# Projecting GQA's gate beside GQA's own attention instead of beside MLA's

## The chip, the cores and the metric

The kernel is one program on one core of a Trainium2 chip. The core has a matrix engine (TensorE, here PE, whose weight loads are shown apart as PEld), a vector engine (DVE), a scalar engine for activations and copies (ACT), a general engine (POOL) and a sync engine that issues the transfers (SP). Each engine works through its own list of instructions; semaphores make one wait for another. The metric is device time in microseconds (us) of one execution.

## The reference, cut to what matters

Two requests (512 and 256 tokens, width 1024) go through two layers with the same weights. Each layer norms its input, projects it, runs four groups of heads side by side, multiplies each group by its own SiLU gate, and projects the result back. All is float32.

```
h = rms_norm(x, norm_g) * (1 + scale) + shift        # scale, shift, gate from ada_w: "ada"
z = h @ w_in                                          # the four groups' inputs and gates ga..gd
oa = mla_branch(...)      # MLA: latents qa, kva -> normed -> up-projected q, k, v; 4 heads
ob = diff_branch(...)     # differential attention
oc = rglru_branch(...)    # recurrence
od = gqa_branch(...)      # GQA: 4 query heads on 2 key heads
o = concat([oa * silu(ga), ob * silu(gb), oc * silu(gc), od * silu(gd)])
x + gate * (o @ w_out)
```

The part that matters here: `od`, its gate `gd`, and MLA's latents and up-projections. `gd` is 256 columns of `w_in`, so a [tokens x 1024] by [1024 x 256] product.

## The kernel before, in words

Every float32 product is made of three products of halves (high and low parts of each operand), by `mm3` (line 286), so almost all matmuls of the profile stand on that line. They write PSUM tiles named acc, s, tr and pv. ACT's copies and activations all stand on line 115 (a helper).

A layer runs in this order. (1) `token_chunk(0)` and `token_chunk(1)` project GQA's q, k, v. (2) GQA's attention: eight jobs (two token groups, four heads), each of them scores into an s tile (L704, L705), row maximum on DVE (L521, L523), exponential on ACT (p<-s,mx), scaling by the row sum, transposes on PE (L538), copies of them to SBUF (pt<-tr), and the product with v (L545). (3) MLA's attention, the same with longer scores (L286, s<-b,b). (4) Recurrence and the differential heads' projections. (5) Differential attention with the other three gates. (6) The output projection.

PE would stand still in an attention while ACT and DVE work on exponentials, so `weave` mixes in other work: a generator `fill`, from which a number of steps is taken after each piece of a job (`F_D` for GQA's attention, `F_A` for MLA's, one number for each layer; `DUE_A` is the starting balance). What is left over is issued behind the attention by `take(fill)`.

- Beside GQA's attention, `fill` is `mla(...)`: six steps of `token_chunk(5)`, the latents of one tile of 128 tokens each, and then six steps that project a tile up (v, then q with its rotation). At the sixth latent step (`UP_AT`) the up-projection's weights wuq and wukv are loaded and split.
- Beside MLA's attention, `fill` is `mixed((3,))`: `gates(3)`, the gate of GQA, in four steps (two halves m of the columns, two token groups), with one chunk of `ada` after each two of them.

`gates(br)` loads and splits the weights of a half (`feat_load`: two transfers, each with an ACT copy into a wh tile and a subtraction on POOL or DVE into a wl tile), makes 24 matmuls for each token group (512 or 256 columns), and evacuates: a tanh on ACT, a scalar_tensor_tensor on DVE, and a multiplication by the attention's output. If the attention's output isn't there yet, the gate is kept in a tile and `gate_mul` multiplies later; the number of DVE operations is the same. wh and wl are pools of six tiles each, acc of two, ws of four; a pool hands out its tiles in the order in which the code asks for them.

The order in which an engine runs its instructions isn't the code's. `arrange` takes the whole program and lists it again: at each step the instruction, on any engine, that could start first by its own table of costs, and among equals the one that comes first in the code. So moving a step in the code changes its rank and the turn of its tiles, and `arrange` then settles where its instructions stand on each engine.

Of the kernel before, what the change touches and what calls it, by code (L numbers as in the profile page):

```python
# [34 lines left out]
GO_D, GO_A, GO_B = ((0, 1), (0, 1), (0, 1))  # L35
KORD = (6, 7, 4, 5, 0, 1, 2, 3)

F_D, F_A, F_B, F_C = ((0.897, 1.178), (0.494, 0.213), (1.2, 1.393), (1.833, 0.976))
MIX_A, MIX_B = (((3,), (3,)), ((0, 2, 1), (2, 0, 1)))
SPL = ((3, 0), (0, 0), (2, 0), None, (3, 1), (0, 1), (2, 1))  # L40
LATE = (3, 4)
LAG_D, LAG_A, LAG_B = ((1, 1), (1, 1), (1, 2))
# [3 lines left out]
PRE_D, PRE_A, PRE_B, UP_AT = ((0, 0), (0, 0), (0, 0), (5, 5))  # L46
# [28 lines left out]
def body(ctx, tc, I, O, dbg=None):  # L75
# [8 lines left out]
    def sb(shape, dt=F32, tag=None, bufs=None):  # L84
        cnt[0] += 1
        nm = f"{tag or 'c'}_{cnt[0]}"
        tag = tag or nm
        return pool.tile(list(shape), dt, name=nm, tag=tag, bufs=bufs or BUFS.get(tag, 1))
# [5 lines left out]
    def ps(tag):  # L94
        cnt[0] += 1
        if tag == "acc":
            rot_acc.append(rot_acc.pop(0))
            tag = rot_acc[-1]
        return ppool.tile([P, 512], F32, name=f"{tag}_{cnt[0]}", tag=tag, bufs=PBUFS[tag])

    def gt(g, box, dt=F32R):

        if g == 0:
            return sb([P, 512], dt, tag="b")
        if not box:
            t = sb([P, 2, 256], dt, tag="b")
            box.extend([t[:, 1], t[:, 0]])
        return box.pop()
# [5 lines left out]
    def act(out, in_, f=AF.Copy, **kw):  # L114
        return nc.scalar.activation(out, in_, f, **kw)  # L115
# [105 lines left out]
    def ada_chunk(l, j, evac, deep):  # L221

        acc = ps("acc")
        for k in range(KC):
            w = deep[j][k] if deep else ada_load(l, j, k, ADA_T[k])
            c = 32 * (k % 4)
            nc.tensor.matmul(acc[c:c + 32], cs[:, k], w, start=(k < 4), stop=(k >= 4))
        evac(acc)
# [23 lines left out]
    def ada_gate(l):  # L252

        for j in range(2):
            c = slice(j * 512, (j + 1) * 512)

            def evac(acc):
                b2 = sb([2, 512], tag="t5")
                nc.sync.dma_start(b2, I["adabg"][l, :, c].to_broadcast([2, 512]))
                row = sb([P, 512], tag="tmp")  # L260
                V.tensor_copy(row, acc)
                rows = ps("acc")
                nc.tensor.matmul(rows[:2], sum4, row, start=True, stop=True)
                V.tensor_tensor(b2, rows[:2], b2, op=ALU.add)
                nc.sync.dma_start(gd[2 * l:2 * l + 2, c], b2)
            ada_chunk(l, 4 + j, evac, None)
            yield

    def load_split(src, n, kg, ncol, tl="wl", th="wh", eng="g"):

        his, los = [], []
        for q in range(n):
            w = sb([P, kg, ncol], tag="ws")
            nc.sync.dma_start(w, src(q))
            hi, lo = split_w(w, [P, kg, ncol], th, tl, eng)
            his.append(hi)
            los.append(lo)
        return his, los
# [91 lines left out]
    for step in START:  # L370
# [8 lines left out]
        else:  # L379
            _, g, hf = step  # L380
# [7 lines left out]
    for l in range(DEPTH):  # L388
# [33 lines left out]
        def token_load(ci):  # L422
            ncol = TCH[ci][1]
            base = sum(c for _, c in TCH[:ci]) * KC
            return load_split(
                lambda q: I["wt"][l, :, base + q * 2 * ncol:base + (q + 1) * 2 * ncol].rearrange(
                    "p (k c) -> p k c", k=2), 4, 2, ncol, eng=EN_T)
# [15 lines left out]
        def feat_load(m):  # L443
            return load_split(
                lambda q: I["wf"][l, m, :, q * 512:(q + 1) * 512].rearrange("p (k c) -> p k c", k=4), 2, 4, P, eng=EN_F)

        def feat_tile(m, evac, loaded=None):

            his, los = loaded or feat_load(m)
            for g, (t0, n) in enumerate(GRP):  # L450
                acc = ps("acc")
                hh, hl = H[g]
                for k in range(KC):
                    mm3(acc[:, :n], his[k // 4][:, k % 4], los[k // 4][:, k % 4], hh[k], hl[k], k == 0, k == KC - 1, "s")
                evac(g, t0, n, acc)
                yield
# [11 lines left out]
        def gate_in(k, g):  # L468
            return og[g][k]


        def gates(br, ahead):
            boxes = [], []
            w = feat_load(2 + 2 * br)
            for m in range(2):
                def evac(g, t0, n, acc):
                    t = sb([P, 512], tag="tmp")
                    act(t[:, :n], acc[:, :n], AF.Tanh, scale=0.5)
                    d = gate_in(2 * br + m, g)
                    if d is None:  # L480
                        d = og[g][2 * br + m] = gt(g, boxes[g], F32)
                        V.scalar_tensor_tensor(d, t[:, :n], 1.0, acc[:, :n], op0=ALU.add, op1=ALU.mult)
                    else:
                        V.scalar_tensor_tensor(t[:, :n], t[:, :n], 1.0, acc[:, :n], op0=ALU.add, op1=ALU.mult)  # L484
                        V.tensor_tensor(d, d, t[:, :n], op=ALU.mult)
                for i, _ in enumerate(feat_tile(2 + 2 * br + m, evac, w)):
                    if i == 0 and m == 0 and ahead:
                        w = feat_load(2 + 2 * br + 1)
                    yield
                if m == 0 and not ahead:  # L490
                    w = feat_load(2 + 2 * br + 1)
# [523 lines left out]
        def split_o(br, g):  # L1015
            f = 0.25 if br == 2 else 0.5
            for k in (2 * br, 2 * br + 1):
                hi, lo, o = *pair(g), og[g][k]
                act(hi, o, AF.Copy, scale=f)
                V.scalar_tensor_tensor(lo, o, f, hi.bitcast(F32), op0=ALU.mult, op1=ALU.subtract)  # L1020
                O2[g][k] = hi, lo
                yield
# [16 lines left out]
        def chain(*gens):  # L1039
            for g in gens:  # L1040
                yield from g
# [6 lines left out]
        def weave(js, fill, per, lag, fine, due=0.0):  # L1048

            for j in js:  # L1050
                j["lag"] = lag
                for _ in push(j):
                    if fine:
                        due += per * (2 / 5 if j["w"] == 2 else 1 / 3)
                        while due >= 1:
                            due -= 1
                            next(fill, None)
                if not fine:
                    due += per * j["w"]
                while due >= 1:  # L1060
                    due -= 1
                    next(fill, None)
# [2 lines left out]
        rot_acc[:] = ROT_A  # L1065
        take(gq)
        rot_acc[:] = ["acc"]
        fill = mla(token_load(5) if PRE_D[l] else None)
        weave(jobs["d"](), fill, F_D[l], LAG_D[l], FINE_D[l], DUE_D[l])
        take(fill)  # L1070
        ada = []
        if l + 1 < DEPTH:
            A, B = (sb([P, KC, 2], tag="ada" + c, bufs=2) for c in "AB")
            ada.append(ada_affine(l + 1, PRA[:, l + 1], A, B))
        ada = chain(*ada, ada_gate(l))

        def mixed(brs, ahead):

            for br in brs:
                gen = gates(br, ahead)  # L1080
                while True:
                    n = 0
                    for _ in range(2):
                        if next(gen, 0) is None:
                            n += 1
                            yield
                    if n == 0:
                        break
                    if next(ada, 0) is None:
                        yield  # L1090
        fill = mixed(MIX_A[l], PRE_A[l])
        weave(jobs["a"](), fill, F_A[l], LAG_A[l], FINE_A[l], DUE_A[l])
        take(fill)
        flush()
# [69 lines left out]
        def rest():  # L1164

            while ga not in posted:
                yield
            if last:
                fnt = sb([P, D], tag="p")
                nc.sync.dma_start(fnt, I["fn"])  # L1170
                fn[:] = fnt[:, :512], fnt[:, 512:]
            yield from split_o(1, ga)
            yield from w_out(ga, 0)

        w0 = w_half(0, [("wl", "wh")] * 4 + [("b", "b")] * 4)
        fill = chain(mixed(MIX_B[l], PRE_B[l]), ada, *[w0 if e is None else split_o(e[0], GO_B[e[1]]) for e in SPL], rest())
# [380 lines left out]
```

## Time and profile before

| what | us |
|---|---|
| median of 3 runs | 940.71 (937.06 to 941.85) |
| the profiled execution | 937.89 |
| its span, first to last instruction | 935.8 |
| PE busy in the span | 876.1 (94%) |
| DVE busy | 651.8 (70%) |
| ACT busy | 545.8 (58%) |
| mean granted TensorE clock, share of full | 0.987 |

2.1 us of the profiled execution lie around its span. A busy PE isn't a PE at its peak: matmuls overlap, the profile counts each from its start to its modelled end, and a matmul that comes alone counts for longer than one in a row of them. The start times of successive matmuls tell what one really takes.

### The profile page before, as it was taken

The numbers are of one execution on the slowest core, as the hardware profiler recorded it, in microseconds if no ns is written. First come the engines' busy times: TensorE is split into PE (matmuls) and PEld (weight loads), VectorE is DVE, ScalarE is ACT, GpSimd is POOL, SyncE is SP. The second block draws the span as 40 slices with busy tenths as digits, with TensorE's granted clock in tenths as the row PEclk, the third lists the DMA queues.
The fourth block names the chain that finished last, engine by engine and source line by source line (L and its number), as shares of the span: only waits on it lengthen the run. The fifth ranks groups of instructions, "written<-read, shape, count | busy, mean of one in ns | idle before, by whom it ended". The sixth has DMA issues, their size and how long they took to land. (4 is left out here: it accounts for less than half of the span.)

```text
span 935.8 us, 15347 instructions
## 1 busy us (share of the span) xinstructions
PE 876.1 (94%) x5248; PEld 689.2 (74%) x5248; DVE 651.8 (70%) x1714; ACT 545.8 (58%) x1331; POOL 147.9 (16%) x168
## 2 busy tenths in 40 slices
PE   4899898999989899999999999999999899999996
PEld 1599666667989665676888986566699888776785
DVE  5677985656298667867656888577435886988645
ACT  5544886766455456655456369688527535778322
POOL 0221011002211010203202111100121131011610
PEclk9999999999999989999999999999999999999999
DMA  9821022213103566237611212020331134325412
GB/s 349 280 75 57 1 68 69 67 52 96 48 21 95 154 198 197 81 98 229 215 46 35 65 38 68 1 68 8 127 105 46 34 93 129 81 72 174 141 46 90
DMA packets 54349, 91.71 MB, mean 98 GB/s; under 512 B 9072, under 2 KB 13936, under 8 KB 54272
## 3 DMA queue, kind: packets, MB, share of 16 engines
q1 hardware_dynamic: 54272, 90.73, 31.3%
q8 instruction: 42, 0.69, 0.3%
q14 instruction: 35, 0.29, 0.1%
HBM read 73.38 MB, written 6.31 MB: 85 GB/s over the span
## 5 line engine op out<-in xcount | busy, mean ns | idle before, releaser
L286 PE MATMUL acc<-wh,b 128*128 128x256 f32 (+4 forms) x720 | 186.9, 307 | 0.0
L286 PE MATMUL acc<-b,wh 128*128 128x512 f32 (+1 forms) x576 | 171.3, 365 | 0.0
L115 ACT ACTIVATE p<-s,mx 128x512 f32<-128x512 f32 (+1 forms) x192 | 118.2, 618 | 47.6 <-DVE mx L521 41.0
L286 PEld LDWEIGHTS acc<-wh,b 128*128 128x128 f32 (+1 forms) x720 | 130.4, 189 | 4.1 <-issue 0.8
L212 POOL TENSOR_TENSOR wl<-ws,wh 128x512 fp32r<-128x512 f32 (+3 forms) x56 | 74.9, 1342 | 369.8 <-ACT wh L115 320.3
L286 PEld LDWEIGHTS acc<-b,wh 128*128 128x128 f32 x576 | 105.4, 191 | 26.7 <-issue 13.7
L286 PE MATMUL acc<-wl,b 128*128 128x256 f32 (+4 forms) x360 | 108.7, 313 | 5.4 <-DVE tmp L1135 1.7
L286 PE MATMUL tr<-wh,b 128*128 128x256 f32 (+2 forms) x432 | 110.6, 289 | 0.0
L286 PE MATMUL acc<-b,wl 128*128 128x512 f32 (+1 forms) x288 | 104.4, 369 | 1.2 <-DVE tmp L484 0.5
L521 DVE TENSOR_REDUCE mx<-s 128x1 f32<-128x512 f32 x128 | 86.4, 683 | 24.7 <-PE s L764 14.6
L115 ACT ACTIVATE wh<-ws 128x512 fp32r<-128x512 f32 (+3 forms) x100 | 63.3, 638 | 40.1 <-PE tr L286 16.1
L538 PE MATMUL tr<-c,p 128*128 128x128 f32 x480 | 82.7, 278 | 3.3 <-DVE p L200 0.9
L538 PEld LDWEIGHTS tr<-c,p 128*128 128x128 f32 x480 | 57.3, 141 | 31.5 <-issue 13.9
L286 PEld LDWEIGHTS tr<-wh,b 128*128 128x128 f32 x432 | 79.6, 190 | 0.7
L286 PEld LDWEIGHTS acc<-wl,b 128*128 128x128 f32 (+1 forms) x360 | 67.2, 189 | 11.0 <-DVE tmp L1135 2.5
L545 PE MATMUL pv<-pt,b 128*64 128x512 f32 (+1 forms) x288 | 72.6, 553 | 1.6 <-ACT pt L115 0.9
L286 PEld LDWEIGHTS acc<-b,wl 128*128 128x128 f32 x288 | 54.6, 191 | 16.6 <-issue 10.9
L115 ACT ACTIVATE pt<-tr 128x512 f32<-128x512 f32 (+1 forms) x120 | 59.6, 511 | 11.4 <-PE tr L538 11.0
L115 ACT ACTIVATE b<-tr 128x128 f32<-128x128 f32 (+7 forms) x92 | 39.5, 448 | 37.5 <-PE tr L286 13.6
L286 PE MATMUL tr<-wl,b 128*128 128x256 f32 (+2 forms) x216 | 61.1, 290 | 0.0
L212 DVE TENSOR_TENSOR wl<-ws,wh 128x512 fp32r<-128x512 f32 (+2 forms) x44 | 36.0, 821 | 32.4 <-ACT wh L115 32.1
L286 PE MATMUL s<-b,b 96*128 96x512 f32 (+2 forms) x192 | 55.4, 392 | 2.5 <-DMA b<-b 2.5
(252 smaller groups left out, 1827.8 us busy)
## 6 DMA issues: line engine op xcount, KB each, us to landing
ws<-wf SPq DMA_DIRECT2D x40, 256.0 KB, 2.8
b<-ada SPq DMA_DIRECT2D x32, 256.0 KB, 5.4
ws<-wt SPq DMA_DIRECT2D x32, 256.0 KB, 2.9
wh<-ada SPq DMA_DIRECT2D x32, 256.0 KB, 4.5
wl<-ada SPq DMA_DIRECT2D x32, 256.0 KB, 4.9
ws<-wo SPq DMA_DIRECT2D x32, 256.0 KB, 3.4
b<-b SPq DMA_DIRECT2D x112, 64.0 KB, 2.0
b<-b SPq DMA_DIRECT2D x112, 32.0 KB, 1.8
```

The costliest lines, as they stand in the source:

```text
L115: return nc.scalar.activation(out, in_, f, **kw)
L212: engine(eng).tensor_tensor(lo, w, hi.bitcast(F32), op=ALU.subtract)
L286: nc.tensor.matmul(out, s, m, start=first and i == 0, stop=last and i == 2)
L521: V.tensor_reduce(mx[:, i:i + 1], views[i], axis=AX.X, op=ALU.min)
L538: nc.tensor.transpose(tr[:, qt * P:(qt + 1) * P], Ps[qt // 2][:, qt % 2, kt * P:(kt + 1) * P], ident)
L545: nc.tensor.matmul(pv[64 * i:64 * i + 64, :n], vt[g][:, k0 + i], pts[i][:, :n], start=(k0 == 0), stop=(k0 + 2 == nk))
```

## The change

`gates(3)` leaves the fill of MLA's attention and is put among MLA's steps beside GQA's attention: after each third step of `mla` one gate step (`GATE_AT`), so after latents 3 and 6 and after up-projections 3 and 6. The fill of GQA's attention has 16 steps in place of 12, and `F_D` goes from 0.897 and 1.178 to 1.2 and 1.5. Beside MLA's attention only ada chunks are left (`ADA_A`: three in the first layer, where there were two, and two in the second, as before); `F_A` goes from 0.494 and 0.213 to 0.3 and 0.2.

```
-F_D, F_A, F_B, F_C = ((0.897, 1.178), (0.494, 0.213), (1.2, 1.393), (1.833, 0.976))
-MIX_A, MIX_B = (((3,), (3,)), ((0, 2, 1), (2, 0, 1)))
+F_D, F_A, F_B, F_C = ((1.2, 1.5), (0.3, 0.2), (1.2, 1.393), (1.833, 0.976))
+MIX_B = ((0, 2, 1), (2, 0, 1))
+GATE_AT, ADA_A = (3, 3), (3, 2)
...
-        fill = mla(token_load(5) if PRE_D[l] else None)
+        def latents():
+            gen = gates(3, 0)
+            for i, _ in enumerate(mla(None)):
+                yield
+                if i % GATE_AT[l] == GATE_AT[l] - 1 and next(gen, 0) is None:
+                    yield
+            yield from gen
+        fill = latents()
         weave(jobs["d"](), fill, F_D[l], LAG_D[l], FINE_D[l], DUE_D[l])
...
+        def some(gen, n):
+            for _ in range(n):
+                if next(gen, 0) is None:
+                    yield
...
-        fill = mixed(MIX_A[l], PRE_A[l])
+        fill = some(ada, ADA_A[l])
         weave(jobs["a"](), fill, F_A[l], LAG_A[l], FINE_A[l], DUE_A[l])
```

No instruction is added or taken away on PE, ACT, DVE or POOL; they are put in another order. The line numbers after the change are one higher than before.

First place: PE, first layer, from MLA's first keys to its first scores (s tiles). acc_2213 before and acc_2204 after are the accumulators of a gate step, wl_/wh_ are its weights, tr_ the transposes, pv the product with v. Before:

```order
L286 MATMUL acc_2213<-b_365,wl_2205 128x512
L286 MATMUL acc_2213<-b_366,wh_2203 128x512
L286 MATMUL acc_2213<-b_365,wh_2203 128x512
L538 MATMUL tr_2147<-c_83,p_1962 128x128 x2
L286 MATMUL acc_2213<-b_376,wl_2205 128x512
L286 MATMUL acc_2213<-b_377,wh_2203 128x512
L286 MATMUL acc_2213<-b_376,wh_2203 128x512
L286 MATMUL acc_2213<-b_387,wl_2205 128x512
L545 MATMUL pv_2141<-pt_2145,b_577 64x256
L545 MATMUL pv_2141<-pt_2150,b_577 64x256
L622 MATMUL tr_2158<-c_83,rot_1843 96x128 x4
L286 MATMUL s_2168<-b_2107,b_2118 128x512
```

After, the rows just ahead of the same scores (the gate step here is the fourth; the third, 24 matmuls of 512 columns, stands earlier, among the up-projections):

```order
L623 MATMUL tr_2299<-c_83,rot_1900 96x128
L287 MATMUL acc_2204<-b_511,wl_2076 128x256
L623 MATMUL tr_2299<-c_83,rot_1900 96x128
L287 MATMUL acc_2204<-b_511,wh_2074 128x256
L623 MATMUL tr_2299<-c_83,rot_1900 96x128
L287 MATMUL acc_2204<-b_511,wh_2074 128x256
L546 MATMUL pv_2282<-pt_2286,b_577 64x256
L546 MATMUL pv_2282<-pt_2291,b_577 64x256
L287 MATMUL acc_2204<-b_519,wl_2082 128x256
L623 MATMUL tr_2299<-c_83,rot_1900 96x128
L287 MATMUL acc_2204<-b_519,wh_2080 128x256
L287 MATMUL s_2309<-b_2248,b_2259 128x512
```

Before, the gate begins at this place and most of its matmuls stand behind the first scores; after, more work lies between the keys and the scores, and the gate is nearly done when they come.

Second place: ACT, first layer, where the up-projection's weights wuq are split (wh<-ws 128x384). Before, they stand ahead of GQA's first exponential:

```order
L115 ACTIVATE wh_1228<-ws_1226 128x640
L115 ACTIVATE wh_1795<-ws_1793 128x384
L115 ACTIVATE t_257_1027<-tr_1002 128x128
L115 ACTIVATE kvh_1807<-ws_1805 128x512
L115 ACTIVATE t_263_1066<-acc_1041 128x128
L115 ACTIVATE wh_1801<-ws_1799 128x384
```

After, the gate's first half has taken the last two of the six wh tiles there, and wuq's splits stand among the exponentials (p<-s,mx):

```order
L116 ACTIVATE p_1804,den_1806<-s_1807,mx_1805 128x512
L116 ACTIVATE b_1201<-tr_1451,c_81 96x128
L116 ACTIVATE pt_1635<-tr_1630 128x512
L116 ACTIVATE b_1203<-tr_1451,c_81 128x128
L116 ACTIVATE wh_1788<-ws_1786 128x384
L116 ACTIVATE pt_1642<-tr_1637 128x512
L116 ACTIVATE b_1199<-tr_1603,c_81 96x128
L116 ACTIVATE b_1201<-tr_1603,c_81 96x128
L116 ACTIVATE wh_1794<-ws_1792 128x384
```

These two splits moved behind thirteen of GQA's score tiles; what the gate's first half puts in their old place are two splits of 128x512.

## Rows read from the trace of the kernel before

**Rows 1.** Windows: start:end length, busy of PE, PEld, DVE, ACT, POOL; clock; DMA
```profile
91.50:133.40 41.90, 39.24 (x230) 29.05 (x229) 37.94 (x131) 37.22 (x111) 2.50 (x7) 1.00 0.09 32
133.40:160.30 26.90, 22.79 (x128) 15.31 (x127) 16.84 (x58) 19.68 (x60) 4.95 (x13) 1.00 0.22 66
160.30:219.30 59.00, 58.92 (x338) 40.50 (x338) 36.68 (x73) 41.26 (x97) 5.08 (x4) 0.97 0.22 65
219.30:305.60 86.30, 82.86 (x619) 76.72 (x616) 57.00 (x111) 44.77 (x93) 15.66 (x20) 1.00 0.22 65
547.90:580.00 32.10, 30.95 (x169) 22.77 (x169) 29.69 (x98) 28.14 (x79) 3.21 (x5) 1.00 0.02 5
580.00:615.30 35.30, 32.79 (x180) 21.60 (x180) 22.34 (x86) 26.63 (x85) 4.19 (x14) 0.95 0.24 78
615.30:660.60 45.30, 45.06 (x261) 28.68 (x259) 32.36 (x69) 38.84 (x96) 1.28 (x1) 1.00 0.12 33
```

**Rows 2.** Lines, forms apart, PE, 91.5 to 160.3 us: count, busy, mean
```profile
L286 PE MATMUL acc<-wh,b 128*128 128x320 f32 x58 | 14.6, 320 | 0.0
L538 PE MATMUL tr<-c,p 128*128 128x128 f32 x76 | 12.7, 280 | 1.1 <-DVE p L200 0.6 <-DVE b L461 0.3
L545 PE MATMUL pv<-pt,b 128*64 128x512 f32 x32 | 10.4, 618 | 0.8 <-ACT pt L115 0.7 <-DVE pt L194 0.2
L286 PE MATMUL acc<-wl,b 128*128 128x320 f32 x28 | 8.3, 321 | 0.0
L704 PE MATMUL s<-b,b 128*128 128x512 f32 x16 | 7.1, 444 | 1.0 <-ACT p L115 1.0
L286 PE MATMUL acc<-wh,b 96*128 96x384 f32 x24 | 6.6, 345 | 0.0
L705 PE MATMUL s<-b,b 128*128 128x512 f32 x16 | 6.4, 400 | 0.0
L286 PE MATMUL acc<-wl,b 96*128 96x384 f32 x12 | 4.5, 377 | 0.5 <-ACT rot L115 0.5
```

**Rows 3.** Timeline, PE alone: start, length, instruction; 117 to 122 us
```profile
117.65 0.40 PE L704 MATMUL s<-b,b 128*128 128x512 f32 x1
117.89 0.31 PE L286 MATMUL acc<-wh,b 128*128 128x320 f32 x1
118.04 0.40 PE L705 MATMUL s<-b,b 128*128 128x512 f32 x1
...
119.68 1.18 PE L545 MATMUL pv<-pt,b 128*64 128x512 f32 x4
120.79 1.09 PE L538 MATMUL tr<-c,p 128*128 128x128 f32 x8
121.64 0.47 PE L704 MATMUL s<-b,b 128*128 128x512 f32 x1
```

**Rows 4.** Timeline, PE alone, 600 to 612 us
```profile
602.99 0.52 PE L286 MATMUL acc<-wh,b 96*128 96x384 f32 x2
603.34 0.34 PE L286 MATMUL acc<-wl,b 96*128 96x384 f32 x1
...
604.66 0.28 PE L705 MATMUL s<-b,b 128*128 128x256 f32 x1
604.78 0.28 PE L286 MATMUL acc<-kvh,b 128*128 128x256 f32 x1
```

**Rows 5.** Waits of PE, 156 to 220 us: total, times, longest
```profile
PE s L286 <- DMA b<-b: 2.5, 1, 2.5
```

**Rows 6.** Windows around that wait
```profile
157.00:160.40 3.40, 0.94 (x9) 0.49 (x5) 1.74 (x3) 1.06 (x3) 0.00 (x0) 1.00 0.52 130
160.40:163.80 3.40, 3.40 (x8) 2.65 (x9) 1.29 (x2) 0.78 (x2) 0.00 (x0) 0.50 0.16 39
```

**Rows 7.** Lines, forms apart, ACT, 160.3 to 219.3 us
```profile
L115 ACT ACTIVATE tmp<-acc 128x512 f32<-128x512 f32 x2 | 1.2, 598 | 2.1 <-PE acc L286 2.1
```

**Rows 8.** Waits of ACT, 611 to 682 us
```profile
ACT tmp L115 <- PE acc L286: 5.9, 2, 5.2
```

## The prediction

> **What bounds the kernel now.** I read the page first, where PE is busy for 94% of the span, then windows over the two attentions of each layer, then PE's lines and start times in them. In GQA's attention of the first layer (91.5 to 160.3 us) PE is idle for 2.7 us in the first part and 4.1 us in the second; in MLA's attention (160.3 to 219.3) for 0.1 us [rows 1]. The second layer's GQA attention has 1.2 and 2.5 us, and the part of its MLA attention up to the last score tile 0.2 [rows 1]. So beside MLA's attention PE has all the work it can take, and beside GQA's it doesn't. What holds PE back there is seen in the same rows: in the first part ACT is busy for 37.2 and DVE for 37.9 of 41.9 us (89% and 91%), in the second for 19.7 and 16.8 of 26.9 (73% and 63%). In the first part the exponentials, row maxima and MLA's latents use up ACT and DVE. In the second none of the engines is full: the up-projections wait for each other's copies.
>
> A busy PE counts overlapping matmuls, so its real load is taken from start times. In rows of each other a 512-column matmul takes 0.24 us and one of 320 columns 0.15, four records of the product with v take 1.11, eight transposes 0.85, or 0.106 each [rows 3]; 384 columns take 0.35/2 = 0.175 and 256 columns 0.12 [rows 4]. The first layer's GQA stretch has 86 of 320 columns (12.9 us), 76 transposes (8.1), 32 records of the product with v (8.9), 32 scores of 512 (7.7) and 36 of 384 (6.3) [rows 2], 43.9 us together. The other 96 of its 358 [rows 1] are smaller; at 0.13, between 0.106 and 0.24, they take 12.5. PE's load is 56.4 of 68.8 us, so 12.4 us are waiting, the 6.8 idle ones among them. The second layer's stretch holds the same work in 67.4 us: 11.4 of waiting.
>
> **The change, part by part.** The gate is 48 matmuls of 512 columns and 48 of 256 in each layer: 48 x 0.24 + 48 x 0.12 = 17.3 us of PE. No instruction of a compute engine goes away, so PE's load over a layer stays. GQA's stretch gets 17.3 us of work and grows by 17.3 - x, where x is waiting that the gate fills; MLA's stretch and what follows it lose 17.3 us and shrink by 17.3 - y, where y is waiting that shows up when the filler is gone. The gain of a layer is x - y.
>
> x, first layer. Just before 160.3 us PE waits 2.5 us for a transfer [rows 5], the rotated part of the keys, which is copied by DMA; MLA's first scores stand at the head of PE's queue and the gate's matmuls behind them. Afterwards about 3 us more work stand between the keys and these scores: some twenty gate matmuls of 256 columns (2.4), an up-projection step (1.4) and a first group of ada matmuls, less the seven gate matmuls of 512 that stood there (1.7). I take 1.9 of the 2.5 as filled; bounds 0 (the ada weights' transfers may hold up this DMA, or the ada matmuls wait for them) and 2.5. Right behind this wait, in which PE is busy for 0.94 of 3.4 us, the granted clock is 0.50 of full, 1.2 in place of 2.4 GHz, for 3.4 us [rows 6]. What was done there took at most half of it longer, 1.7 us, which goes with the wait. Of the other 9.9 us of waiting I take half, 5.0: those of the second part lie open, since ACT and DVE have room, while those of the first part come from ACT and DVE, which the gate loads further. Bounds 0 and 9.9. x = 1.9 + 1.7 + 5.0 = 8.6.
>
> x, second layer. There's no such DMA wait. The clock is 0.95 over 35.3 us [rows 1], so half for some 3.5 us: 1.8. Of the other 9.6 again half: x = 1.8 + 4.8 = 6.6.
>
> The Trainium skill has another measure of PE's room: "Perfetto Trace Analysis", section "Identifying the Most-Contended Engine", says that matmul busy time misleads and that the busy share of weight loads shows the headroom. Here loads are busy for 44.4 of 68.8 us beside GQA's attention (64%), and for 76.7 of 86.3 (89%) in the dense stretch behind MLA's [rows 1]. By that rule the gate's 96 loads, at 76.7/616 = 0.125 us each, would bring the stretch to 56.4 us of loads, which at 89% fit into 63 us: it wouldn't grow at all. Start times say 56.4 + 17.3 = 73.7 us at the least, for products with v and 512-column matmuls take long without loads; I go by them, and the rule stands as a rival.
>
> y. MLA's attention in the first layer would be 59.0 - 15.6 (all gate matmuls but the seven) = 43.4 us. ACT is busy there for 41.3 us [rows 1], less two tanh passes of 0.6 [rows 7] and two half ones, 2.0 by estimate: 39.3 us, 90% of 43.4. The second layer's MLA stretch has ACT at 38.8 of 45.3, 86%, and lets PE idle for 0.2 [rows 1]: at 86% it takes 45.7, so y = 2.3. In the second layer only a few gate matmuls stand inside the attention and most behind it, at a place with nothing to wait for; y = 0.7. Bounds: 0, and the idle rate of GQA's stretch (6.8 of 68.8) over 45 us, 4.4.
>
> The moves at no cost: the gate's evacuations go with it. ACT gets 2.0 us more in a stretch with 56.9 of 68.8 used, and DVE about as much; in the first part they aren't free, which is why only half of the waiting was taken. The splits of wuq go from ahead of GQA's first exponential to behind the thirteenth score tile, two of about 0.6 us at most (an ACT pass over 512 columns, [rows 7]); two splits of the gate take their place. What waits for them is the first up-projection, and gate matmuls and attention stand in PE's queue ahead of it; if that cover is gone, a copy and a subtraction show, 1 to 2 us a layer. On SP's queue the gate's weights go ahead of wuq's at a time when DMA is used to 0.09 [rows 1]. One ada chunk moves in the first layer from differential attention to MLA's: between a gain and a loss of 2 us, taken as 0.
>
> The sum: 937.9 (the profiled execution) - (8.6 + 6.6) + (2.3 + 0.7) = 925.7 us. The median of the runs, 940.7, is 2.8 above the profiled one; 925.7 + 2.8 = 928.5, so 929.
>
> **The rivals.** The waiting only moves (B): y comes to about x, because exponentials, maxima and transposes wait for each other in any attention, and the filler hides it wherever it stands. For it: in the first part of GQA's stretch ACT and DVE are at about 90% with PE idle, and MLA's stretch comes to 90% of ACT. Against it: the second layer's MLA stretch at 86%, with 0.2 us idle. Price: 940.
>
> ACT and DVE set the pace (C, slower): PE's waits in GQA's attention belong to a full ACT, the gate's tanh passes and the late wuq splits make it longer, and x is 0, while MLA's stretch, without filler, waits like GQA's now, y = 4.4 in both layers: 937.9 + 8.8 + 2.8 = 949.5, so 950. It decides from the point where y exceeds x. For it: a tanh that waits for a gate's sum kept ACT idle for up to 5.2 us at one place in the second layer [rows 8]; among GQA's exponentials that would hold them up. Against it: the gate's steps stand between latents whose copies wait in the same way, and the second part has room. The Trainium skill, "TensorE: Matmul & The Clock Gate", section "Architectural detail: the array is 16× 32×32, not 1× 128×128", says that ACT and DVE work strictly in order, which is what that 5.2 us wait looks like.
>
> All of it is filled (D): x is the whole waiting, 12.4 + 1.7 and 11.4, and y is 0: 937.9 - 25.5 + 2.8 = 915. For it: weight loads are busy for only 44.4 of the 68.8 us [rows 1]; against it: ACT and DVE in the first part. By the Trainium skill's rule on weight loads alone, with x = 17.3 in both layers and y = 3.0 in all, it would be 909.
>
> That the change doesn't do what it says, because the planner had pulled the gate ahead already, is excluded by the order: before, only seven gate matmuls of the first layer stand ahead of MLA's scores.
>
> **How the numbers follow.** Forecast A 0.56, B 0.24, C 0.14, D 0.06. A's own range, with a quarter to three quarters of the open waiting filled: 5 us either way, 923 to 935. I call no change what lies within 0.5% of 940.7, 936.0 to 945.4, about what a measurement of this kernel can tell. All of A and D and a quarter of B are faster: 0.68. The rest of B but a little, and the mild end of C, are the same: 0.19. Slower: 0.13. The range 918 to 945 leaves out D's lower part and most of C.
>
> **What would show it.** Right: GQA's stretches (first GQA score to first MLA score) grow from 68.8 and 67.4 to about 77.5 and 77 us with PE idle under 4; MLA's stretch of the first layer falls from 59.0 to about 45, PE idle under 2.5; the wait for the DMA at MLA's first scores and the half clock behind it are gone. B: GQA's stretches grow less or as much, and PE idles by 4 us or more in MLA's. C: GQA's stretches over 85 us with ACT over 85% busy. Wrong in another way: a first up-projection waiting for wuq's split, or ada matmuls that wait for their weights ahead of the scores.

## The result and the profile after

| | before | after |
|---|---|---|
| median of the runs, us | 940.62 | 927.40 (924.91 to 929.65) |
| ratio, 95% interval | | 0.9872 [0.9837, 0.9907] |
| the profiled execution, us | 937.89 | 926.08 |
| its span, us | 935.8 | 924.2 |

The change takes 13.2 us off, by the interval 8.7 to 15.3; 929 was forecast. The page's first lines after (span; busy time, share, instructions):

```profile
span 924.2 us, 15331 instructions
PE 870.7 (94%) x5248; PEld 685.9 (74%) x5248; DVE 648.8 (70%) x1714; ACT 547.0 (59%) x1331; POOL 149.3 (16%) x168
```

PE's share is 94% as before, and ACT and DVE did the same work, so the page's shares don't show the gain. Windows by stage do. Those after, with the limits of [rows 1] (the first two are the first layer's GQA attention, the third its MLA attention, the fourth what follows up to differential attention's first score; then the same four of the second layer):

```profile
93.50:139.60 46.10, 45.55 (x270) 34.87 (x269) 39.43 (x140) 40.20 (x115) 4.31 (x8) 1.00 0.12 36
139.60:169.90 30.30, 29.46 (x172) 21.58 (x172) 16.17 (x54) 19.36 (x59) 3.69 (x12) 1.00 0.18 52
169.90:219.70 49.80, 49.57 (x298) 31.22 (x297) 35.70 (x75) 39.23 (x95) 5.59 (x8) 1.00 0.41 133
219.70:311.00 91.30, 86.93 (x630) 80.26 (x628) 60.59 (x116) 47.30 (x96) 15.46 (x15) 0.98 0.24 71
540.30:573.90 33.60, 33.11 (x192) 26.27 (x192) 29.09 (x100) 27.81 (x79) 2.46 (x6) 1.00 0.03 9
573.90:620.00 46.10, 43.76 (x256) 30.78 (x255) 28.46 (x94) 32.19 (x95) 5.53 (x15) 1.00 0.26 82
620.00:668.20 48.20, 47.41 (x257) 27.46 (x256) 34.93 (x72) 39.74 (x94) 5.20 (x8) 1.00 0.26 76
668.20:765.80 97.60, 93.68 (x676) 86.24 (x674) 62.73 (x121) 51.72 (x104) 20.02 (x19) 1.00 0.20 57
```

Two stretches of before reach further than those shown ahead of the prediction, up to differential attention's first score:

```profile
219.30:314.70 95.40, 89.71 (x653) 82.29 (x649) 60.40 (x121) 47.73 (x97) 15.66 (x20) 1.00 0.26 76
660.60:779.70 119.10, 113.50 (x772) 99.67 (x770) 70.58 (x133) 57.09 (x113) 24.97 (x27) 0.99 0.26 77
```

| stretch, us | layer 1 before | after | | layer 2 before | after | |
|---|---|---|---|---|---|---|
| GQA's attention | 68.8 | 76.4 | +7.6 | 67.4 | 79.7 | +12.3 |
| MLA's attention | 59.0 | 49.8 | -9.2 | 45.3 | 48.2 | +2.9 |
| from there to differential attention | 95.4 | 91.3 | -4.1 | 119.1 | 97.6 | -21.5 |
| the rest of the layer | 233.2 | 229.3 | -3.9 | 156.1 | 158.4 | +2.3 |

With 2.0 us more ahead of the first score, these make up the span's 11.6. The gate takes 17.3 us of PE in a layer. GQA's attention grew by 7.6 and 12.3, so 9.7 and 5.0 us would have gone into waiting (x) if just those 17.3 us had crossed into it. PE's matmuls in the two traces, counted in these stretches, say what crossed. In the first layer seven of the gate's 512-column matmuls had stood there before and ten of 256 columns stand behind it after, so 14.4 us of the gate crossed; with eight matmuls of ada more (0.9) and three of the latents fewer (0.5) that is 14.8, and 7.2 us went into waiting. In the second layer nine of the gate's had stood there (2.2 us), and eight of ada (0.9) and four of the product with v (1.1) came in with it: 17.1 us crossed, and 4.8 went into waiting.

PE's idle time in GQA's attention fell from 6.8 to 1.4 us in the first layer and from 3.7 to 2.8 in the second. Beside MLA's attention PE idles for 0.2 us in the first layer (before 0.1) and 0.8 in the second (before 0.2). In the second layer the last stretch has 96 matmuls less. That this is also the gate's number is chance: 20 of them are ada's, and 17 matmuls of the stretch's other projections stand beside MLA's attention after. The gate had not all stood behind the attention there. Its first two steps, of four, are evacuated by the end of MLA's attention in the trace before (ACT's timeline):

```profile
643.69 0.59 ACT L115 ACTIVATE tmp<-acc 128x512 f32<-128x512 f32 x1
663.80 0.36 ACT L115 ACTIVATE tmp<-acc 128x256 f32<-128x256 f32 x1
```

At MLA's first scores in the first layer the wait for the key's transfer [rows 5] and the half clock behind it [rows 6] are gone. PE's waits after, 160 to 220 us, and windows around the place:

```profile
PE acc L228 <- ACT rot L116: 0.3, 1, 0.3
PE acc L287 <- ACT rot L116: 0.2, 1, 0.2
```
```profile
166.00:170.00 4.00, 3.69 (x28) 2.23 (x28) 1.45 (x3) 1.89 (x5) 0.92 (x3) 1.00 0.74 204
170.00:174.00 4.00, 4.00 (x26) 3.55 (x25) 2.68 (x6) 2.63 (x8) 0.00 (x0) 1.00 0.99 332
```

DMA is busy to 0.74 while the keys are copied; PE has 28 matmuls to do meanwhile, and its clock stays at 1.00 of full.

### The profile page after: what moved, and what is told of

It is laid out like the page before. It is cut to its first block, busy times and chain, and to the rows that moved or that the text cites. A ratio compares the mean times of both kernels' runs of the same rounds, so it can differ in the third digit from the quotient of the medians.

```text
span 924.2 us, 15331 instructions
## 1 busy us (share of the span) xinstructions
PE 870.7 (94%) x5248; PEld 685.9 (74%) x5248; DVE 648.8 (70%) x1714; ACT 547.0 (59%) x1331; POOL 149.3 (16%) x168
## 5 line engine op out<-in xcount | busy, mean ns | idle before, releaser
L213 POOL TENSOR_TENSOR wl<-ws,wh 128x512 fp32r<-128x512 f32 (+3 forms) x56 | 75.2, 1348 | 318.7 <-ACT wh L116 233.2
L287 PEld LDWEIGHTS acc<-b,wh 128*128 128x128 f32 x576 | 103.4, 189 | 22.9 <-issue 11.2
L287 PEld LDWEIGHTS tr<-wh,b 128*128 128x128 f32 x432 | 79.7, 190 | 0.7
L116 ACT ACTIVATE pt<-tr 128x512 f32<-128x512 f32 (+1 forms) x120 | 59.2, 512 | 21.5 <-PE tr L539 20.7
L546 PE MATMUL pv<-pt,b 128*64 128x512 f32 (+1 forms) x288 | 69.3, 549 | 0.1
```

Source lines behind the costliest of these rows:

```text
L213: engine(eng).tensor_tensor(lo, w, hi.bitcast(F32), op=ALU.subtract)
L287: nc.tensor.matmul(out, s, m, start=first and i == 0, stop=last and i == 2)
L546: nc.tensor.matmul(pv[64 * i:64 * i + 64, :n], vt[g][:, k0 + i], pts[i][:, :n], start=(k0 == 0), stop=(k0 + 2 == nk))
```

## The experiments

Each kernel was timed beside runs of the kernel before on the same chip, in three groups: one layer at a time, the pace alone and two ada chunks (median of before 940.26 us); the key's transfer alone and the three places of the gate (939.19); and the last, with both edits at once, the missing transfer in the changed kernel, and the change and two chunks again (939.54). Ratios are to the runs of before in the group.

**1. One layer at a time.** The change in the first layer, the second as before; and the other way round.

```
-F_D, F_A, ... = ((1.2, 1.5), (0.3, 0.2), ...
+F_D, F_A, ... = ((1.2, 1.178), (0.3, 0.213), ...
-        fill = latents()
+        fill = latents() if l == 0 else mla(None)
-        fill = some(ada, ADA_A[l])
+        fill = some(ada, ADA_A[l]) if l == 0 else mixed((3,), 0)
```

Expected of the first layer alone: 

> The gate moves beside GQA's attention in the first layer alone; the second layer is as before. Theory T (the gate fills PE's waits beside GQA's attention, and each layer gives its own part): 5 to 8 us faster than before, 933 to 936, the wait for the key transfer at MLA's first scores gone and no half clock there. Rival P (the gain is the planner's luck with the order as a whole, or one layer's alone): either nothing, 939 to 942, or the whole 13 us, 927 to 929.

Measured: 934.01 us, 0.9946 [0.9922, 0.9970], 6.25 us less.

Expected of the second layer alone: 

> The gate moves in the second layer alone. Theory T: 5 to 8 us faster than before, 933 to 936, so that the two layers' gains add up to the 13 us of the whole change within 3. Rival P: nothing, 939 to 942, or the whole, 927 to 929.

Measured: 933.65 us, 0.9939 [0.9913, 0.9966], 6.6 us less. Together that is 12.85, the change's 13.2 within the intervals: each layer gains for itself, by about the 6.3 and 5.9 us of the prediction's x - y. With the first layer as before, PE's wait for the key's transfer is still there, and a half clock behind it (the wait's total, times and longest, then a window):

```profile
PE s L287 <- DMA b<-b: 2.7, 1, 2.7
```
```profile
160.70:163.40 2.70, 2.70 (x7) 2.12 (x8) 0.69 (x1) 0.40 (x1) 0.00 (x0) 0.50 0.20 49
```

No trace of experiments 1 to 4 that lacks this wait has a half clock between 150 and 220 us.

**2. The pace alone.** The kernel before with the change's `F_D`; the gate stays beside MLA's attention.

```
-F_D, ... = ((0.897, 1.178), ...
+F_D, ... = ((1.2, 1.5), ...
```

Expected: 

> The kernel before with the new pace of GQA's fill alone (F_D 1.2 and 1.5 in place of 0.897 and 1.178); the gate stays beside MLA's attention. Theory T: no change, within 3 us of before, since the same steps fill the same stretch. Rival Q (latents and up-projections taken sooner are what brings the gain): 6 us or more faster, below 935.

Measured: 936.96 us, 0.9971 [0.9951, 0.9991], 3.3 us less, between the two theories. So part of the gain can be had without moving the gate. In its trace PE has no wait at all between 150 and 220 us. The up-projections start earlier (the first at 116.7 us, before at 126.7), but the last stands where it did, and the keys are not copied earlier. Their first transfer is issued 1.7 us later (SP's timeline, first before, then with the new pace):

```profile
154.45 0.60 SPq L916 DMA_DIRECT2D b<-b  x1
```
```profile
156.13 0.59 SPq L916 DMA_DIRECT2D b<-b  x1
```

What differs is the work on PE ahead of MLA's first scores: from 155.7 us on, four of GQA's score matmuls and eleven of the gate's stand there, before only seven of the gate's, and the scores start at 159.9 us without a wait, before at 160.3.

**3. The key's transfer alone.** The kernel before, with the rotated part of the first layer's first keys set to 0 in place of being copied.

```
+                    if l == 0 and g == 0 and p == 0:
+                        G.memset(kh[64:96].bitcast(F32), 0.0)
+                        G.memset(kl[64:96].bitcast(F32), 0.0)
+                    else:
                         nc.sync.dma_start(kh[64:96]..., kp[:32]...)
                         nc.sync.dma_start(kl[64:96]..., kp[32:64]...)
```

Expected: 

> The kernel before, where the rotated part of the first layer's first keys (first token group, first head pair) is set to zero by POOL in place of four transfers, so that PE's 2.5 us wait at MLA's first scores has no cause; this leaves out that part of the keys. Theory T (this wait and the half clock behind it are 3.6 us of the first layer's gain): 2.5 to 4.5 us faster than before. Rival S (that time is only shifted: the exponentials behind these scores end when they did): within 1.5 us of before.

Measured: 934.93 us, 0.9951 [0.9933, 0.9968], 4.3 us less. Then the same edit in the changed kernel. Expected: 

> The change as it is, but the rotated part of the first layer's first keys is set to 0 by POOL instead of being copied by DMA (it leaves out that part of those keys). The kernel before gained 4.3 us by this edit. T (the change has already filled that wait, and the half clock behind it): the same time as the change, 926 to 928.5 us. S (the change's gain comes from elsewhere, the key's transfer still sets when MLA's first scores start): again 4 us faster, 922 to 924 us.

Measured: 927.98 us, 0.9900 [0.9867, 0.9933], beside 926.85 for the change itself in the same group: nothing more to gain. The change has filled this wait. What it is worth before is less sure than the 4.3 us of the medians: in the profile, from GQA's first score to differential attention's first, the first layer is some 2.3 us shorter than before (220.8 for 223.2), and 1.2 more come off in the second layer, which the edit doesn't touch.

**4. Pace and transfer together.** Are 2 and 3 one gain or two? Expected: 

> The kernel before with the change's pace of GQA's fill alone (1.2 and 1.5 for 0.897 and 1.178), and the first layer's first rotated keys set to 0 by POOL instead of copied by DMA (it leaves out that part of those keys). Apart, the pace brought 3.3 us and the missing copy 4.3 us. T (the faster pace gains only by issuing the keys earlier, so that other work stands between them and the first scores: both edits take away one wait): 934.5 to 936.5 us, no further than either alone. P (the pace has a gain of its own, an earlier up-projection): the two add up, 931 to 933 us.

Measured: 938.58 us, 0.9995 [0.9974, 1.0017], outside what either theory gave: no gain at all. The stretch in question agrees with T. Windows of its trace around MLA's first scores, to be held against [rows 6]:

```profile
157.00:160.40 3.40, 3.40 (x20) 2.65 (x20) 2.65 (x4) 2.58 (x8) 2.02 (x5) 1.00 0.42 127
160.40:163.80 3.40, 3.40 (x18) 2.29 (x17) 2.94 (x7) 2.23 (x7) 0.00 (x0) 1.00 0.13 33
```

There is no wait and no half clock, and from the first to the last MLA exponential it takes 59.7 us, with the pace alone 59.5, before 62.0. From GQA's first score to differential attention's first the first layer takes 223.2 us before, 220.5 with the pace, 220.8 without the transfer and 220.5 with both: the two edits take away one wait, as T has it, though not by issuing the keys earlier (experiment 2). But the span is 2.0 us longer than with the pace alone, 0.9 of them ahead of GQA's first exponential and 1.3 behind the second layer's MLA attention, at places that neither edit touches. At the second place the profile with both edits has a half clock that the one with the pace alone lacks (first the pace alone, then both):

```profile
732.00:740.00 8.00, 5.79 (x41) 5.37 (x40) 5.34 (x16) 6.72 (x11) 0.63 (x1) 1.00 0.31 100
```
```profile
732.00:740.00 8.00, 5.82 (x28) 5.16 (x29) 4.36 (x16) 5.88 (x9) 0.58 (x1) 0.79 0.32 100
```

That explains the profiles in part; why the median over all runs shows no gain was not settled. It also says that a 3 us difference of a single edit of this kind isn't to be trusted to the microsecond.

**5. The place of the gate's steps beside GQA's attention.** The same 12 steps of `mla`, with the gate's four steps at other places: behind steps 1 to 4 (early), 6, 8, 10 and 12 (late), or all four behind the last up-projection (last).

```
-GATE_AT, ADA_A = (3, 3), (3, 2)
+GATE_AT, ADA_A = ((0, 1, 2, 3), (0, 1, 2, 3)), (3, 2)     # early
+GATE_AT, ADA_A = ((5, 7, 9, 11), (5, 7, 9, 11)), (3, 2)   # late
+GATE_AT, ADA_A = ((11,), (11,)), (3, 2)                   # last
-                if i % GATE_AT[l] == GATE_AT[l] - 1 and next(gen, 0) is None:
+                if i in GATE_AT[l] and next(gen, 0) is None:
```

Expected of late: 

> The kernel after with the gate's four steps behind the last latent and the second, fourth and sixth up-projection, in place of behind each third step. Theory T (in the first part of GQA's attention ACT and DVE are full and the gate finds less waiting than in the second): 0 to 5 us faster than after, 922 to 927. Rival U (the gate fills waiting in the first part as well, where PE is idle for 2.7 us): 2 to 5 us slower than after, 929 to 932.

Measured: 927.42 us, 0.9883 [0.9851, 0.9915].

Expected of early: 

> The kernel after with the gate's four steps behind the first four latents, all in the first part of GQA's attention. Theory T: slower than after by 4 to 10 us, 931 to 937, the wait for the key transfer back at MLA's first scores and the second part's idle time as before. Rival U: within 3 us of after, 924 to 930.

Measured: 927.74 us, 0.9883 [0.9861, 0.9904]. Late and early take the same time as the change, so U holds for early, and late lies between its two theories. In the early version the gate's evacuations in the first layer (ACT's timeline: start, length) show that it is done by the end of the part of GQA's attention in which ACT and DVE had been at 89% and 91% [rows 1]. Three of the four steps stand in that part; of the first step's 24 matmuls 20 stand ahead of GQA's first score, and in exchange 39 matmuls of the latents, which in the change are ahead of it, stand in the attention:

```profile
95.43 0.58 ACT L116 ACTIVATE tmp<-acc 128x512 f32<-128x512 f32 x1
108.96 0.39 ACT L116 ACTIVATE tmp<-acc 128x256 f32<-128x256 f32 x1
123.79 0.60 ACT L116 ACTIVATE tmp<-acc 128x512 f32<-128x512 f32 x1
137.95 0.37 ACT L116 ACTIVATE tmp<-acc 128x256 f32<-128x256 f32 x1
```

Its windows over the two parts of that attention:

```profile
94.80:140.00 45.20, 44.29 (x266) 34.19 (x264) 34.45 (x106) 35.26 (x92) 5.22 (x7) 1.00 0.08 24
140.00:173.60 33.60, 32.52 (x207) 24.69 (x203) 22.52 (x85) 24.97 (x83) 4.05 (x14) 1.00 0.39 118
```

ACT is at 78% in the first part, since latents moved out to the second, and PE idles for 0.9 us. From GQA's first exponential to differential attention's, the first layer takes 221.9 us, in the change 214.8. Some of this is work (38 more of the latents' matmuls, 5.7 us, and 19 fewer of the gate's and other projections, at most 4.6), and up to 3.4 is the clock: 10.2 us of it are at half clock, in the change 3.4. Ahead of it and behind it this version is faster (94.8 us for 97.4, 101.7 for 103.4 in differential attention, and in the second layer's MLA attention 48.5 for 50.4), and the time at the end is the same.

Expected of last: 

> The kernel after with all four gate steps behind the last up-projection, but still ahead of MLA's attention in the code. Theory T: about half of the gain lost, 930 to 936: the key transfer's wait is covered, the waits among the up-projections only as far as the planner pulls the gate ahead. Rival V (the code's order says little, since the planner moves the gate wherever PE waits): within 2 us of after, 925 to 930.

Measured: 952.04 us, 1.0145 [1.0123, 1.0168], 13 us slower than before; no theory had that. Windows of 20 us over its first layer's GQA attention and the start of MLA's:

```profile
115.00:135.00 20.00, 17.26 (x90) 11.28 (x88) 17.22 (x61) 16.27 (x49) 4.19 (x5) 0.98 0.18 52
135.00:155.00 20.00, 18.20 (x91) 11.75 (x88) 9.31 (x38) 13.28 (x40) 2.02 (x7) 0.77 0.00 1
155.00:175.00 20.00, 19.65 (x106) 15.81 (x105) 5.40 (x17) 5.86 (x19) 1.84 (x6) 1.00 0.30 94
175.00:195.00 20.00, 17.82 (x100) 8.29 (x99) 9.62 (x16) 8.53 (x22) 2.54 (x2) 1.00 0.81 258
```

From 155 to 195 us ACT and DVE do a quarter to a half of a window's work: PE runs the gate as one block while the attention stands still. ACT's timeline there (in brackets the idle time before, and what ended it):

```profile
165.15 0.60 ACT L116 ACTIVATE tmp<-acc 128x512 f32<-128x512 f32 x1 [4.71 <-PE acc L287]
173.48 0.38 ACT L116 ACTIVATE tmp<-acc 128x256 f32<-128x256 f32 x1 [7.73 <-PE acc L287]
```

And the part ahead of it, from which the gate had been taken, waits as before: PE idles for 4.5 us from 115 to 155, and its clock falls to half in the second 20 us (0.77, so half for 9.2). Behind the gate something else differs: 40 matmuls of ada, in the change 8, stand ahead of MLA's first scores. In part they no longer run four at a time, and they wait for a transfer (PE's timeline):

```profile
182.34 1.04 PE L228 MATMUL acc<-wh,c 128*32 128x512 f32 x2
183.01 1.04 PE L228 MATMUL acc<-wl,c 128*32 128x512 f32 x2
187.64 1.04 PE L228 MATMUL acc<-wl,c 128*32 128x512 f32 x2 [1.18 <-DMA wl<-ada]
```

From GQA's first to differential attention's first exponential this version takes 233.4 us, the change 214.8. PE's idle time and clock over these stretches, first this version, then the change:

```profile
96.60:330.00 233.40, 220.67 (x1365) 169.20 (x1364) 149.90 (x377) 143.45 (x357) 28.95 (x43) 0.98 0.22 68
```
```profile
97.40:312.30 214.90, 208.91 (x1349) 165.40 (x1351) 149.03 (x376) 143.10 (x357) 29.06 (x43) 0.99 0.25 76
```

Of the 18.6 us, 6.7 are PE's idle time (12.7 and 6.0) and up to 3.4 the half clock (10.2 us of it and 3.4); the other 8.5 lie in matmuls that the profile counts as busy. Most of these have a cause in the trace: 16 more projection matmuls stand in this version's stretch, up to 3.8 us, and ada's matmuls take 12.0 us there from each start to the next, in the change 6.7, with the wait of 1.2 among them. So the same filler, which gains *between* the attention's pieces, loses where the code gives it as a block ahead of MLA's scores, with ada drawn in behind it. How much of the loss is the block alone isn't shown.

**6. The third ada chunk.** The change with two chunks beside the first layer's MLA attention, as before.

```
-GATE_AT, ADA_A = (3, 3), (3, 2)
+GATE_AT, ADA_A = (3, 3), (2, 2)
```

Expected: 

> The kernel after with two ada chunks beside MLA's attention in the first layer in place of three, as before. Theory T: within 2 us of after, 925 to 930. Rival R (the chunk taken out of the differential attention is a good part of the gain, as the 3.9 us that this attention became shorter in the profile suggest): 3 us or more slower than after, 930 or more.

Measured: 924.35 us, 0.9843 [0.9815, 0.9872]. Then both on one chip. Expected of the change again: 

> The change itself, to stand beside the version with two ada chunks on the same chip: 926 to 928.5 us.

Expected of two chunks again: 

> The change with two ada chunks beside MLA's attention in the first layer, as before, in place of three. If the third chunk costs something there, 2 to 4 us below the change on the same chip, 923.5 to 926 us; if the first measurement (924.35) was chance, within 1 us of the change.

Measured: 926.85 us, 0.9871 [0.9848, 0.9894], and 923.85, 0.9854 [0.9824, 0.9884]: 3.0 us apart by the medians, as the first time (3.05). The intervals overlap. By the means of the six runs each it is 1.6 us here (926.7 and 925.1), since two runs with two chunks took 928.6 and 928.8, longer than any with three. Both comparisons have the same sign; the size is 1.6 to 3 us. Windows of both traces over the first layer's MLA attention, what follows, and differential attention (limits at the exponentials). Three chunks:

```profile
171.30:223.60 52.30, 52.06 (x311) 32.52 (x309) 36.66 (x77) 42.21 (x104) 5.60 (x8) 1.00 0.36 116
223.60:312.40 88.80, 83.89 (x612) 77.97 (x615) 58.99 (x112) 43.74 (x87) 15.47 (x15) 0.98 0.25 74
312.40:418.10 105.70, 99.77 (x537) 67.53 (x530) 77.78 (x156) 63.01 (x162) 14.32 (x11) 0.97 0.41 121
```

Two:

```profile
170.50:220.40 49.90, 49.76 (x297) 32.46 (x297) 37.40 (x77) 42.73 (x106) 5.29 (x8) 1.00 0.25 78
220.40:307.40 87.00, 82.65 (x606) 76.67 (x604) 56.14 (x111) 43.29 (x85) 14.16 (x15) 0.98 0.27 76
307.40:412.10 104.70, 99.40 (x547) 68.27 (x540) 77.55 (x157) 61.20 (x159) 12.80 (x10) 0.97 0.48 139
```

The third chunk costs 2.4 + 1.8 = 4.2 us where PE is full. Taken back to differential attention, that stretch doesn't grow (it is 1.0 shorter), and the next one, up to the second layer's first exponential, grows by 2.5. The version with two chunks has the lowest median of all that ran.

## Why the prediction was right

**The terms.** The gain of a layer as x - y came out at its size (6.3 and 5.9 against 6.25 and 6.6 measured apart). The prediction let the whole 17.3 us of the gate cross from one stretch to the other, though it counted seven matmuls that stood in GQA's stretch already; what is given too much to x by that is given too much to y, and the gain isn't touched. By what crossed:

- x, first layer: 8.6 was forecast. 7.2 of the waiting in GQA's stretch were filled, and up to 1.7 come from the half clock, which lies behind that stretch: 7.2 to 8.9. The wait, taken as 1.9 of 2.5, is all filled; the 4.7 that remain of the 7.2 are about the half of the other 9.9 that was taken (5.0).
- x, second layer: 6.6 was forecast, 4.8 filled. The half clock is gone (1.00 over both parts, before 0.95 in the second), and its 1.8 are among the 4.8. So some 3 of the other 9.6 were filled, where the half, 4.8, had been taken.
- y, first layer: 2.3 was forecast. With two ada chunks, as before (experiment 6), MLA's attention and what follows are 16.8 us shorter (137.6 for 154.4). 15.3 us of matmuls left, and up to 1.7 are the half clock, so y is about 0.
- y, second layer: 0.7 was forecast. By the profile of the kernel before it is -1.3, 17.3 - (21.5 - 2.9). That "only a few gate matmuls stand inside the attention" was a wrong reading, since about half did, and "a place with nothing to wait for" was wrong too. Before, that stretch had a wait in which PE was busy for 3.9 of 6 us, and then the half clock, which the changed kernel's 97.6 us don't have:

```profile
730.00:736.00 6.00, 3.90 (x29) 3.31 (x27) 5.96 (x14) 2.65 (x4) 3.29 (x3) 1.00 0.02 3
736.00:741.50 5.50, 4.99 (x20) 4.37 (x21) 2.69 (x11) 3.58 (x6) 0.00 (x0) 0.69 0.43 140
```

  That half clock is no fixed part of the kernel: of the five profiles that leave the second layer's gate where it was, three have none at this place. From MLA's first score to differential attention's first these five take 162.9 to 164.4 us there, the change 145.7, so y lies between 0.1 and -1.3.
- The ada chunk, "between a gain and a loss of 2 us, taken as 0", costs 1.6 to 3 net. That it and the overestimated y offset each other is luck.

**The step that failed** is the reason given for "half": that the waiting of the second part lies open, "while those of the first part come from ACT and DVE, which the gate loads further". In the changed kernel half of the gate, 8.6 us, stands in the first part (its tanh passes start at 107.5 and 139.3 us); that part is only 4.2 us longer, and PE's idle time in it fell from 2.7 to 0.55 us. The early version puts three of the four steps there and loses nothing at the end. The 89% and 91% were those of the attention *and* MLA's latents, which can move. In the early version some of them go to the second part, and ACT is at 78%; in the change itself it is still at 87% (40.2 of 46.1 us), so a high share of ACT did not keep PE from filling its waits.

**The signs named ahead.** GQA's attention: about 77.5 and 77 forecast, 76.4 and 79.7 measured, PE idle under 4: right. The transfer's wait and the half clock behind it: gone, right. MLA's attention of the first layer: about 45 forecast, 49.8 measured. 338 matmuls before, less 89 of the gate, would be 249; there are 298. Ten are the end of the gate, 8 are more of ada, 16 are ada's small sums (8 of the third chunk, 8 that stood behind), and 14 are projections that stood behind. So about half of the surplus was drawn in from the stretch behind, which is shorter for it. A stretch's end isn't a wall for the planner, and the sum of both stretches was the better sign. "Wrong in another way" didn't come: in the first layer's GQA attention PE waits for no weight split, and an ada matmul waits for 0.3 us.

**The rivals.** B (the waiting only moves) is out: PE's idle time beside MLA's attention is 0.2 and 0.8 us. C (ACT and DVE set the pace) is out in the change, but the version with all four steps last has the waits that C names: ACT waits for gate sums for 4.7 and 7.7 us, and the time is 13 us over before. D and the rule of the Trainium skill on weight loads ("Perfetto Trace Analysis", "Identifying the Most-Contended Engine") are out: GQA's attention, with loads busy for 64% of it, wasn't free for what came in, but grew by 7.6 and 12.3. Load by start times gave 73.7 us as the least, 76.4 were measured; but that it was so close has luck in it, since not all of the 17.3 us crossed. With what crossed the least is 56.4 + 14.8 = 71.2 us in the first layer and 56.0 + 17.1 = 73.1 in the second (79.7 measured), so 5 and 7 us of waiting are left.

**What is open**: how much of the 13.2 us is the faster pace by itself (it gains 3.3 before, and in the first layer it removes the wait that the moved gate removes too), what the new pace of MLA's fill does by itself, why experiments 2 and 3 together gain nothing in the median, and how much of the loss of the version with all four steps last is the block alone.

## What to carry to other kernels

Put filler where the engine that sets the pace waits, and take its room there from the start times of instructions, not from busy shares: the stretches grew to their load so reckoned plus 5 and 7 us. Count the work that really crosses into a stretch; filler often stands partly there already. A high share of a second engine in one part of a stretch isn't a wall if movable work makes up some of it. The filler gained here where it stood between the pieces of the work that it hides; the same filler as a block, with ada's matmuls drawn in behind it, cost 25 us against the interleaved one. Even a small piece has a price in a stretch that is already full (4.2 us there, 1.6 to 3 at the end), so look at each piece that a change moves along with the main one.

## What the runs showed of the hardware

- The granted clock's half stretches aren't at the same places in two profiles of one kernel. The same 19 matmuls of the changed kernel, first in the profile above, then in the one of experiment 6, where they come 1.9 us later:

```profile
836.00:842.00 6.00, 4.36 (x19) 2.89 (x19) 3.84 (x9) 3.29 (x11) 0.00 (x0) 0.72 0.47 133
```
```profile
837.90:842.00 4.10, 2.92 (x19) 2.07 (x20) 3.39 (x9) 2.80 (x10) 0.00 (x0) 1.00 0.36 84
```

  PE had 1.2 GHz for 3.4 us in one and 2.4 throughout in the other, and the stretch took 6.0 us for 4.1. A difference of 1 to 2 us between two single profiles can be no more than that.
- The ada matmuls, which write 32 partitions each at four different places of a tile, ran four at a time: four start within 0.02 us, and the next four 0.45 us later, 0.11 us for one in place of the 0.24 of a 512-column matmul onto 128 partitions [rows 3]. PE's timeline after:

```profile
177.81 0.62 PE L228 MATMUL acc<-wh,c 128*32 128x512 f32 x1
177.82 0.62 PE L228 MATMUL acc<-wl,c 128*32 128x512 f32 x1
177.82 0.62 PE L228 MATMUL acc<-wh,c 128*32 128x512 f32 x1
177.83 0.62 PE L228 MATMUL acc<-wl,c 128*32 128x512 f32 x1
178.26 0.59 PE L228 MATMUL acc<-wh,c 128*32 128x512 f32 x1
```

  A chunk has 16 such records (3 chunks make 48) and 8 small ones for its sums. The 16 are 1.8 us of PE by these starts, and the chunk cost 4.2 in the full stretch. What the rest is wasn't tried; that they don't always run four at a time shows in the version with all four gate steps last, where pairs of them started 0.67 us apart (182.34 and 183.01), 0.33 for one.
